# Taps of a depthwise convolution moved out of the B and C convolutions of an SSD, with four staging buffers for the memory products

## The chip, the cores and the metric

One core of one Trainium2 chip. The time is device microseconds (us) of one execution, as the median of several runs. A profile comes from one further, profiled execution. The engines are called PE (TensorE; PEld is its weight loading), DVE (VectorE), ACT (ScalarE), POOL (GpSimd) and SP (SyncE, which issues the transfers).

## What is computed

One decoder layer on 1024 tokens of width 1024, in float32 throughout. Cut to what matters here:

```
u = rms_norm(h); P = u @ W_in       # [conv GLU | z, x, B, C, dt | q, k, v | 3 gates]
y_A = conv_branch(...)              # a * sigmoid(gate), depthwise causal conv of 31 taps, LayerNorm, swish, W_A
y_B = ssd_branch(...)               # causal conv of 4 taps on x, B, C; chunked scan; silu(z); grouped norm; W_B
y_C = swa_branch(...)               # sliding-window attention
h += (sig(g_A)*y_A + sig(g_B)*y_B + sig(g_C)*y_C) @ W_mix
h += memory_cross_attention(rms_norm(h), rms_norm(mem))
h += relu(rms_norm(h) @ W_up)**2 @ W_down

# inside ssd_chunked, per group of 8 heads and chunk of 128 tokens
scores = (C @ B^T) * decay                      # decay = exp of differences of cumulated dt * a
y  = scores @ (x * dt)  +  (C @ state) * exp(cs)
state = state * exp(cs_end) + (B * decay_to_end)^T @ (x * dt)
```

## The kernel before

Every product of float32 operands is made of three matmuls on rounded halves: an operand is split into a high half (`wh`, `uh`) and a remainder (`wl`, `ul`), and hi*hi, hi*lo and lo*hi are added up in PSUM. A weight slot (`wslot`, L139 to L156) loads 128x1024 numbers into a staging tile `ws` (pool `wst`, 2 buffers), ACT rounds it into `wh` (L154) and POOL subtracts to get `wl` (L155); the halves come from the pool `wp`, of 3 buffers. `gemm_ch` (L191) makes 128 output channels of all 1024 tokens of it, in 8 steps of 6 matmuls with 512 columns.

The order on PE is the order of the program. Other engines get theirs from a scheduler, which may bring loads, casts and elementwise work forward; weight slots have high priority. Work that should lie between the matmuls is put in by hand: `step()` (L91) runs after a part of a product, and takes from a list of side jobs the first one that is due (`after(n, fn)` makes one due n steps from now). With each step it may also emit one tap of the depthwise convolution.

The taps: `convolve` (L316 to L335) is a generator. For each of 8 tiles of 128 channels it loads the GLU's result into `hin` (with POOL's memset of the left edge and ACT's first tap into `tapy`, L326), yields four times empty, and then emits 30 multiply-adds on DVE (L331, 128x1024 elements), one per yield. `pace[0]` says how often a step asks for one: with pace 2 every second step, with 3 every third, with 0 never. There is one `hin`, so a tile's load waits for the last tap of the tile before.

The stages:

- First (0 to about 125 us): x is loaded and split, three gate tiles are multiplied with the not yet normalised x as it comes (`ps_g`), the square sums give the norms of x and of the memory (`token_rstd`, L244; its steps are named `xn_...` and `mn_...`). Then the keys and values of the memory are made (`ps_kv`, L436 to L469): 16 weight slots of two loads of w_xkv of 256 KB each. Two of five of them take their halves from a pool `wkv` of WKV = 2 buffers, the others from `wp`, so there are five places for halves in all, and two staging tiles. Beside these products `normalise` (L410 to L421, due after 3 steps) multiplies x by its norm and splits it again: per tile DVE multiplies, ACT casts (`uh`) and DVE subtracts (`ul`).
- Second (about 125 to 640 us): the GLU tiles, k and v, q, z (L699 to L720). Taps run here with pace 2 (GLU, z) or 3 (k, v, q).
- SSD (about 640 to 1250 us): for each of four groups g there are four convolutions of 4 taps on x (`conv4`, L738: the product, an eviction by ACT into `c4v`, a first tap on ACT, three on DVE, L746, tanh on ACT, and DVE's L751), each turned to tokens by PE some 10 steps later (`to_tok`, L754, `ps_tok`). Then `b_and_c(g+1)` (L866) makes the next group's B and C in the same way, and `core(g)` (L774) does the chunks: PE multiplies C by the state (`ps_yo`), makes the state's increment (`ps_stt`) and the diagonal part (`ps_yd`); DVE copies or adds the state (L821, L819). `prepare(c)` loads the differences of the cumulated sums (`csb`), makes 8 relus and an exponential on ACT, masks them by `cbm` on DVE (L790), and makes `xd` (DVE, L792) and `xe` (POOL). Chunks 0 and 1 are prepared at the start of `core`, chunk c + 2 at the end of chunk c. Between the chunks `fill` makes parts of the gate tiles (`ps_g`). Taps run with pace 2 everywhere except in `core`, where the pace is 0.
- Then attention, the output products, the cross-attention and the MLP, which the change does not touch.

Of the kernel before, what the change touches and what calls it, by code (L numbers as in the profile page):

```python
# [17 lines left out]
P = 128  # L18
# [11 lines left out]

TURN, TURN_TOK, TURN_Y = 18, 10, 14
TURN_XQ = 8
WKV = 2
GCOL = 512


# [20 lines left out]
def trunk_kernel(tc, w_io):  # L57
# [3 lines left out]
    with ctx:  # L61
# [21 lines left out]
        side = []  # L83
        steps_done = [0]
        taps = [iter(())]
        pace = [0]

        def after(n, fn):
            side.append((steps_done[0] + n, fn))
# [1 line left out]
        def step():  # L91

            steps_done[0] += 1
            if pace[0] and steps_done[0] % pace[0] == 0:
                next(taps[0], 0)
            for i, (due, fn) in enumerate(side):
                if due <= steps_done[0]:
                    side.pop(i)
                    fn()
                    break  # L100
# [35 lines left out]
        d_bv = dram.tile([16, 384], F32, name="d_bv")  # L136
        d_skew = dram.tile([16, P * 385], F32, name="d_skew")

        def wslot(src, first=False, pool_=None):  # L139
            with ExitStack() as e:  # L140
                if not first:
                    e.enter_context(tc.high_priority())
                st = wst.tile([P, 1024], F32, tag="ws", name="ws")
                if isinstance(src, list):
                    for n, part in enumerate(src):
                        nc.sync.dma_start(
                            st.rearrange("p (k n c) -> p k n c", k=2, n=2)[:, :, n, :],
                            part.rearrange("p (k c) -> p k c", c=256),
                        )
                else:  # L150
                    nc.sync.dma_start(st, src)
                wh = (pool_ or wp).tile([P, 1024], F32R, tag="wh", name="wh")
                wl = (pool_ or wp).tile([P, 1024], F32R, tag="wl", name="wl")
                act.copy(wh, st)  # L154
                pool.tensor_sub(wl, st, wh.bitcast(F32))  # L155
            return wh, wl  # L156
# [117 lines left out]
        with ExitStack() as s1:  # L274
# [62 lines left out]
            with ExitStack() as sc:  # L337
# [58 lines left out]
                for i in range(NRAW):  # L396
# [7 lines left out]
                        else:  # L404
                            act.copy(th[:, h * 512:h * 512 + 512], fps[i][h])
                    raw.append(th)
                rm = token_rstd(xp, macc, M, 1.0 / D, EPS, "mn")
                pe.on = True

                def normalise():  # L410

# [18 lines left out]
                xv = xp.tile([P, 2, D], F32, name="xv")  # L430
                kt = memt.rearrange("p a b -> p (a b)").rearrange("p (a b) -> p a b", a=2)
                ss = xp.tile([P, 4, 2], F32, name="kss")
                wk = sc.enter_context(tc.tile_pool(name="wkv", bufs=WKV))
                after(3, normalise)
                after(26, raw_gates)
                for s in range(4):  # L436

                    ps = pg.tile([P, T], F32, tag="g", name="ps_kv").rearrange("p (a b) -> p a b", b=512)
                    for kp in range(4):
                        wh, wl = wslot(  # L440
                            [w_io["w_xkv"][s * 2 + n, kp // 2][:, kp % 2 * 512:kp % 2 * 512 + 512] for n in range(2)],
                            pool_=(wk, wk, None, None, None)[(s * 4 + kp) % 5],
                        )
                        for kk in range(2):
                            k = kp * 2 + kk
                            c = slice(kk * 512, kk * 512 + 512)
                            for tt in range(2):
                                a, b = mh[:, k, tt * P:(tt + 1) * P], ml[:, k, tt * P:(tt + 1) * P]
                                pe.matmul(ps[:, tt, :], a, wh[:, c], start=k == 0, stop=False)
                                pe.matmul(ps[:, tt, :], b, wh[:, c], start=False, stop=False)  # L450
                                pe.matmul(ps[:, tt, :], a, wl[:, c], start=False, stop=k == KT - 1)
                            step()
                    for tt in range(2):
                        to = kt if s < 2 else xv
                        v = to[:, tt, s % 2 * 512:s % 2 * 512 + 512]
                        act.activation(v, ps[:, tt, :], AF.Copy, scale=rm[:, tt:tt + 1])
                        if s < 2:
                            for h in range(2):
                                junk = x2.tile([P, 256], F32, tag="kjunk", name="kjunk", bufs=1)
                                act.activation(  # L460
                                    junk, v[:, h * 256:h * 256 + 256], AF.Square,
                                    accum_out=ss[:, s * 2 + h, tt:tt + 1],
                                )
                    if s == 1:
                        rk = rsqrt_small(xp, ss.rearrange("p a b -> p (a b)"), 8, 1.0 / 256, EPS, "rk")
                        for h in range(4):
                            for tt in range(2):
                                v = kt[:, tt, h * 256:(h + 1) * 256]
                                dve.tensor_scalar(v, v, rk[:, h * 2 + tt:h * 2 + tt + 1], None, ALU.mult)  # L469
# [26 lines left out]
            with ExitStack() as sc:  # L496
# [199 lines left out]
                            d_skew[h].rearrange("(q i) -> q i", i=385)[:, :384], d_bv[h].partition_broadcast(P)  # L696
                        )
                after(8, distances)
                pace[0] = 2  # L699
                glu(1)  # L700
                pace[0] = 3
                tm512(w_io["w_kv"], 0, keys_values)
                pace[0] = 2
                glu(2)
                pace[0] = 3
                tm512(w_io["w_q"], 0, queries_of(0))
                pace[0] = 2
                glu(3)
                pace[0] = 3
                tm512(w_io["w_q"], 1, queries_of(1))  # L710
                pace[0] = 2
                glu(4)
                tm512(w_io["w_z"], 0, z_of(0))
                steps()
# [9 lines left out]
            with ExitStack() as sc:  # L724
# [47 lines left out]
                    )  # L772

                def core(g, ctt):  # L774
                    state = None
                    ops = {}

                    def prepare(c):
                        col = c * 32 + g * HPG
                        hs = slice(col, col + HPG)  # L780
                        cb = fp.tile([P, HPG, P], F32, tag="csb", name="csb")
                        nc.sync.dma_start(
                            cb, d_cs[c, g * HPG:(g + 1) * HPG, :].rearrange("h q -> (h q)").partition_broadcast(P)
                        )
                        for r in range(HPG):
                            act.activation(
                                cb[:, r, :], cb[:, r, :], AF.Relu, bias=csc[:, col + r:col + r + 1], scale=-1.0
                            )
                        act.activation(cb, cb, AF.Exp, scale=-1.0)
                        dve.tensor_mul(cb, cb, cbm[:, c, :].unsqueeze(1).to_broadcast([P, HPG, P]))  # L790
                        xd = fp.tile([P, GCOL], F32, tag="xd", name="xd")
                        dve.tensor_mul(h3(xd), h3(xtok[:, c, :]), hb(dts[:, hs]))  # L792
                        xe = None
                        if c < NT - 1:
                            xe = fp.tile([P, GCOL], F32, tag="xe", name="xe")
                            pool.tensor_mul(h3(xe), h3(xtok[:, c, :]), hb(dtd[:, hs]))
                        pool.tensor_mul(h3(xtok[:, c, :]), h3(xtok[:, c, :]), hb(C("d_skip", g * HPG, HPG)))
                        ops[c] = cb, xd, xe

                    prepare(0)  # L800
                    prepare(1)
                    for c in range(NT):
# [28 lines left out]
                            dve.tensor_add(y, y, yo)  # L831
                        dve.tensor_add(y, y, pyd)
                        if c + 2 < NT:
                            prepare(c + 2)

                def finish(g):
# [33 lines left out]
                def turn_b(ctt):  # L870
                    to_tok(bt, btok)
                    for o in range(2):
                        after(TURN_TOK + o, lambda o=o: cb_of(ctt, o))

                ctt = b_and_c(0)
                turn_b(ctt)
                for g in range(4):
                    for j in range(4):
                        to_tok(
                            conv4(g * 4 + j), xtok[:, :, j * P:(j + 1) * P], (g - 1) * 4 + j if g else None  # L880
                        )
                    if g < 3:
                        following = b_and_c(g + 1)
                    else:
                        fill(TURN_TOK + 1)
                    pace[0] = 0
                    core(g, ctt)
                    pace[0] = 2
# [562 lines left out]
```

## Time and profile before

| | |
|---|---|
| median of 3 runs | 2826.53 us (2825.64 to 2829.45) |
| the profiled execution, its time / its span | 2829.2 us / 2827.4 us |
| mean granted clock of PE | 0.988 |
| idle time of PE in the span | 72.9 us |
| DVE, ACT, POOL busy | 50%, 36%, 30% |
| transfers | 267.22 MB, mean 95 GB/s |

The page gives busy times, a table of 40 slices and groups of instructions. A row of a timeline has the start in us, the duration, the engine, the line and operation, what is written and read, and in brackets the idle time of the engine before it with what ended it. "x4" is a run of four instructions, whose duration is that of the whole run. A row of the waits has who waited for whom, the total in us, how many times and the longest. A row of windows has the stretch and its length, the busy time (and instruction count) of PE, PEld, DVE, ACT and POOL, then the granted clock, the busy share of the DMA engines and GB/s.

### The profile page before, as it was taken

What the parts mean: (1) busy time and instruction counts of PE and PEld (TensorE: products, weight loads), DVE (VectorE), ACT (ScalarE), POOL (GpSimd) and SP (SyncE); (2) the same over time, 40 slices, a digit from 0 to 9 for tenths busy, and PEclk for the clock granted to TensorE, in tenths of its full rate; (3) what the DMA queues carried; (4) which work ended last, traced back from release to release, by engine and by line L of the source; (5) the groups of instructions that cost most, each with busy time, mean ns of one, the idle gap of its engine ahead of it and who ended that gap; (6) DMA issues with size and microseconds to landing.
All of it is one profiled execution on the core that took longest, in us unless ns stands there. A gap on an engine that the chain in (4) does not pass through costs nothing. (4 is left out here: it accounts for less than half of the span.)

```text
span 2827.4 us, 31802 instructions
## 1 busy us (share of the span) xinstructions
PE 2754.5 (97%) x12892; PEld 2221.7 (79%) x12892; DVE 1423.9 (50%) x1610; ACT 1004.3 (36%) x1662; POOL 843.2 (30%) x376
## 2 busy tenths in 40 slices
PE   8899999999899989999999999999999999999999
PEld 6688878888687868775578878899778888888887
DVE  6556667659788887755424674323342222222222
ACT  6523321124455546446612351336432211122111
POOL 4522221202526261524342332321142222222221
PEclk9999999999999999999999999999999999999999
DMA  6552232321333333352354332311111111111111
GB/s 215 183 143 90 88 119 94 103 89 60 103 114 107 102 104 120 114 188 83 101 201 163 113 105 89 105 53 39 45 45 45 45 52 46 45 53 45 53 45 75
DMA packets 94516, 267.22 MB, mean 95 GB/s; under 512 B 9105, under 2 KB 34081, under 8 KB 93985
## 3 DMA queue, kind: packets, MB, share of 16 engines
q1 hardware_dynamic: 94368, 265.19, 28.3%
q8 instruction: 101, 1.65, 0.2%
q14 instruction: 47, 0.38, 0.0%
HBM read 210.47 MB, written 57.83 MB: 95 GB/s over the span
## 5 line engine op out<-in xcount | busy, mean ns | idle before, releaser
L155 POOL TENSOR_TENSOR wl<-ws,wh 128x1024 fp32r<-128x1024 f32 x200 | 502.2, 2513 | 1387.1 <-ACT wh L154 1327.3
L74 PE MATMUL ps_g<-oh,wh 128*128 128x512 f32 x1792 | 563.1, 396 | 4.2 <-ACT oh L1037 4.2
L74 PE MATMUL ps_g<-ol,wh 128*128 128x512 f32 x1792 | 556.2, 392 | 3.7 <-DVE ol L1038 3.4
L74 PE MATMUL ps_g<-oh,wl 128*128 128x512 f32 x1792 | 553.8, 390 | 0.0
L154 ACT CAST wh<-ws 128x1024 fp32r<-128x1024 f32 x200 | 209.7, 1049 | 885.7 <-PE ps_g L74 777.3
L331 DVE SCALAR_TENSOR_TENSOR tapy<-hin,cst,tapy 128x1024 f32<-128x1024 f32 x240 | 396.2, 1651 | 30.7 <-ACT tapy L326 25.0
L74 PEld LDWEIGHTS ps_g<-oh,wh 128*128 128x128 f32 x1792 | 335.7, 188 | 80.8 <-issue 7.1
L74 PEld LDWEIGHTS ps_g<-ol,wh 128*128 128x128 f32 x1792 | 335.9, 188 | 80.3 <-DVE ol L1038 9.4
L74 PEld LDWEIGHTS ps_g<-oh,wl 128*128 128x128 f32 x1792 | 336.9, 188 | 72.0
L74 PE MATMUL ps_g<-uh,wh 128*128 128x512 f32 x1008 | 332.2, 408 | 9.3 <-ACT uh L350 8.2
L74 PE MATMUL ps_g<-ul,wh 128*128 128x512 f32 x1008 | 326.0, 398 | 0.1
L74 PE MATMUL ps_g<-uh,wl 128*128 128x512 f32 x1008 | 317.4, 394 | 1.7 <-POOL wl L155 1.7
L74 PEld LDWEIGHTS ps_g<-ul,wh 128*128 128x128 f32 x1008 | 191.1, 190 | 50.4 <-issue 9.3
L74 PEld LDWEIGHTS ps_g<-uh,wl 128*128 128x128 f32 x1008 | 191.0, 190 | 43.6 <-POOL wl L155 2.9
L74 PEld LDWEIGHTS ps_g<-uh,wh 128*128 128x128 f32 x1008 | 179.9, 191 | 38.3 <-ACT uh L350 8.2
L1341 DVE TENSOR_TENSOR ht<-ht,ps_g 128x1024 f32<-128x1024 f32 x64 | 78.2, 1222 | 250.2 <-PE ps_g L74 250.2
L74 PE MATMUL ps_tm<-wh,uh 128*128 128x512 f32 x448 | 175.7, 392 | 0.0
L74 PE MATMUL ps_tm<-wh,ul 128*128 128x512 f32 x448 | 174.6, 390 | 0.0
L74 PE MATMUL ps_tm<-wl,uh 128*128 128x512 f32 x448 | 174.4, 389 | 0.0
L1331 DVE SCALAR_TENSOR_TENSOR relu<-ps_g,rb 128x1024 f32<-128x1024 f32 x32 | 39.2, 1225 | 221.8 <-PE ps_g L74 221.8
L169 POOL TENSOR_TENSOR wl<-ws,wh 128x1024 fp32r<-128x1024 f32 x28 | 70.6, 2532 | 230.2 <-ACT wh L168 230.2
L746 DVE SCALAR_TENSOR_TENSOR c4a<-c4v,cst,c4a 128x1023 f32<-128x1023 f32 (+2 forms) x72 | 96.9, 1345 | 10.4 <-ACT c4a L744 9.0
(341 smaller groups left out, 3436.2 us busy)
## 6 DMA issues: line engine op xcount, KB each, us to landing
ws<-w_ch SPq DMA_DIRECT2D x64, 512.0 KB, 3.6
csb<-d_cs SPq DMA_DIRECT2D x32, 512.0 KB, 3.8
gth<-d_th SPq DMA_DIRECT2D x32, 512.0 KB, 4.4
ws<-w_up SPq DMA_DIRECT2D x32, 512.0 KB, 3.3
ws<-w_down SPq DMA_DIRECT2D x32, 512.0 KB, 3.3
d_th<-gate_th SPq DMA_DIRECT2D x21, 512.0 KB, 5.1
ws<-w_xkv SPq DMA_DIRECT2D x32, 256.0 KB, 3.1
ws<-w_z SPq DMA_DIRECT2D x16, 512.0 KB, 3.4
```

Of the source, the lines that this page charges most:

```text
L74: ins = nc.tensor.matmul(*a, **k)
L154: act.copy(wh, st)
L155: pool.tensor_sub(wl, st, wh.bitcast(F32))
L169: pool.tensor_sub(wl[:, :, c], s3, wh[:, :, c].bitcast(F32))
L331: dve.scalar_tensor_tensor(y, hin[:, j:j + T], w(j), y, ALU.mult, ALU.add)
L746: dve.scalar_tensor_tensor(a[:, s:], v[:, :T - s], C("c4_w", ct * 4 + 3 - s), a[:, s:], ALU.mult, ALU.add)
L1331: dve.scalar_tensor_tensor(r, ps, 0.0, rb, ALU.max, ALU.mult)
L1341: dve.tensor_add(hv, hv, ps)
```

## The change

- The memory products take one of four weight slots from the pool `wkv` (now of one buffer), the others from `wp`: four places for halves in place of five. Every second slot is staged in a tile of `wkv` instead of `wst`, with two buffers: four staging tiles in place of two.
- The norm of the memory (`mn`) becomes a side job that is due after one step, in place of standing ahead of the products.
- The pace becomes a fraction: each step adds it to `owed`, and a tap is emitted when that reaches 1. In the second stage it is 0.6 throughout (before 1/2 and 1/3), in the SSD 0.5 as before, and 0 from `b_and_c(g+1)` on (for the last group, from the `fill` in its place) to the end of `core`.
- `prepare` is cut in two: `exps(c)` loads `csb` and makes relus and exponential; for the first two chunks it is a side job, 2 and 6 steps into `b_and_c(g+1)`. For the others it stands at the old place, ahead of `prepare(c + 2)`.

```diff
             steps_done[0] += 1
-            if pace[0] and steps_done[0] % pace[0] == 0:
+            owed[0] += pace[0]
+            if owed[0] >= 1:
+                owed[0] -= 1
                 next(taps[0], 0)
...
-        def wslot(src, first=False, pool_=None):
+        def wslot(src, first=False, pool_=None, stage=None):
...
-                st = wst.tile([P, 1024], F32, tag="ws", name="ws")
+                st = (stage or wst).tile([P, 1024], F32, tag="ws", name="ws", bufs=2 if stage else None)
...
-                rm = token_rstd(xp, macc, M, 1.0 / D, EPS, "mn")
                 pe.on = True
+                rms = []
+                after(1, lambda: rms.append(token_rstd(xp, macc, M, 1.0 / D, EPS, "mn")))
...
-                wk = sc.enter_context(tc.tile_pool(name="wkv", bufs=WKV))
+                wk = sc.enter_context(tc.tile_pool(name="wkv", bufs=1))
...
-                            pool_=(wk, wk, None, None, None)[(s * 4 + kp) % 5],
+                            pool_=wk if (s * 4 + kp) % 4 == 0 else None, stage=wk if kp % 2 else None,
...
-                pace[0] = 2
+                pace[0] = 0.6
                 glu(1)
-                pace[0] = 3
                 tm512(w_io["w_kv"], 0, keys_values)
...
+                    pace[0] = 0
+                    do = core(g, ctt)
+                    for c in range(2):
+                        after(2 + 4 * c, lambda c=c: do.exps(c))
                     if g < 3:
                         following = b_and_c(g + 1)
                     else:
                         fill(TURN_TOK + 1)
-                    pace[0] = 0
-                    core(g, ctt)
-                    pace[0] = 2
+                    do.run()
+                    pace[0] = 0.5
                     finish(g)
```

How the instructions move is shown at three places. The first is DVE in group 0 of the SSD, from the last steps of the first x convolution (`c4a`, of four steps each) to the third; `tapy` rows are taps, `cbm` and `csb` the mask and the masked decays. Before:

```order
L751 SCALAR_TENSOR_TENSOR c4a<-c4v,c4a 128x1024
L331 SCALAR_TENSOR_TENSOR tapy<-hin,cst,tapy 128x1024
L769 TENSOR_TENSOR cbm<-ps_cb,mat 128x512
L790 TENSOR_TENSOR csb<-csb,cbm 128x1024
L746 SCALAR_TENSOR_TENSOR c4a<-c4v,cst,c4a 128x1023
L746 SCALAR_TENSOR_TENSOR c4a<-c4v,cst,c4a 128x1022
L746 SCALAR_TENSOR_TENSOR c4a<-c4v,cst,c4a 128x1021
L751 SCALAR_TENSOR_TENSOR c4a<-c4v,c4a 128x1024
L331 SCALAR_TENSOR_TENSOR tapy<-hin,cst,tapy 128x1024 x3
```

The same place of DVE now:

```order
L747 SCALAR_TENSOR_TENSOR c4a<-c4v,c4a 128x1024
L332 SCALAR_TENSOR_TENSOR tapy<-hin,cst,tapy 128x1024
L765 TENSOR_TENSOR cbm<-ps_cb,mat 128x512
L332 SCALAR_TENSOR_TENSOR tapy<-hin,cst,tapy 128x1024
L790 TENSOR_TENSOR csb<-csb,cbm 128x1024
L332 SCALAR_TENSOR_TENSOR tapy<-hin,cst,tapy 128x1024 x2
L742 SCALAR_TENSOR_TENSOR c4a<-c4v,cst,c4a 128x1023
L742 SCALAR_TENSOR_TENSOR c4a<-c4v,cst,c4a 128x1022
L742 SCALAR_TENSOR_TENSOR c4a<-c4v,cst,c4a 128x1021
L747 SCALAR_TENSOR_TENSOR c4a<-c4v,c4a 128x1024
L332 SCALAR_TENSOR_TENSOR tapy<-hin,cst,tapy 128x1024 x4
```

Between the first and second convolution stand four taps where one stood, since the four empty yields between two channel tiles of the taps have moved; behind the second, four where three stood.

The second place is DVE in the same group, from the end of the last x convolution to the state of the first chunk; `bt` is B's last step, and the `c4a` rows behind it are C's. Before:

```order
L331 SCALAR_TENSOR_TENSOR tapy<-hin,cst,tapy 128x1024 x4
L746 SCALAR_TENSOR_TENSOR c4a<-c4v,cst,c4a 128x1023
L792 TENSOR_TENSOR xd<-xtok,dtmp_dt 128x512
L746 SCALAR_TENSOR_TENSOR c4a<-c4v,cst,c4a 128x1022
L792 TENSOR_TENSOR xd<-xtok,dtmp_dt 128x512
L746 SCALAR_TENSOR_TENSOR c4a<-c4v,cst,c4a 128x1021
L751 SCALAR_TENSOR_TENSOR bt<-c4v,c4a 128x1024
L331 SCALAR_TENSOR_TENSOR tapy<-hin,cst,tapy 128x1024 x4
L746 SCALAR_TENSOR_TENSOR c4a<-c4v,cst,c4a 128x1023
L746 SCALAR_TENSOR_TENSOR c4a<-c4v,cst,c4a 128x1022
L821 COPY state<-ps_stt 128x512
```

The same place of DVE now:

```order
L742 SCALAR_TENSOR_TENSOR c4a<-c4v,cst,c4a 128x1023
L792 TENSOR_TENSOR xd<-xtok,dtmp_dt 128x512
L742 SCALAR_TENSOR_TENSOR c4a<-c4v,cst,c4a 128x1022
L792 TENSOR_TENSOR xd<-xtok,dtmp_dt 128x512
L742 SCALAR_TENSOR_TENSOR c4a<-c4v,cst,c4a 128x1021
L747 SCALAR_TENSOR_TENSOR bt<-c4v,c4a 128x1024
L742 SCALAR_TENSOR_TENSOR c4a<-c4v,cst,c4a 128x1023
L742 SCALAR_TENSOR_TENSOR c4a<-c4v,cst,c4a 128x1022
L830 COPY state<-ps_stt 128x512
```

The eight taps are gone from this stretch; all else is in its old order.

The third place is the start of the program on SP, where `ws` rows are loads of weights and `xt` rows loads of x. Before:

```order
L108 DMA cst<-consts 128x582
L151 DMA ws<-w_ch 128x1024
L349 DMA xt<-xT 128x1024
L151 DMA ws<-w_ch 128x1024
L349 DMA xt<-xT 128x1024 x2
L151 DMA ws<-w_ch 128x1024
L146 DMA ws<-w_xkv 128x2x256 x2
```

The same place of SP now:

```order
L147 DMA ws<-w_xkv 128x2x256 x4
L109 DMA cst<-consts 128x582
L152 DMA ws<-w_ch 128x1024
L350 DMA xt<-xT 128x1024
L152 DMA ws<-w_ch 128x1024
L350 DMA xt<-xT 128x1024
L152 DMA ws<-w_ch 128x1024
```

The four loads for the new staging tiles, which wait for nothing, have moved to the head of the queue. The loads of `csb` and the relus and exponentials of the first two chunks stand at nearly the same places on SP and ACT as before, where the scheduler had already put them ahead.

More of the change, by code (lines that the diff above doesn't have):

```diff
@@ L32 @@
 TURN_XQ = 8
-WKV = 2
 GCOL = 512
@@ L85, in trunk_kernel @@
         taps = [iter(())]
-        pace = [0]
+        pace, owed = [0], [0]
         def after(n, fn):
@@ L455, in trunk_kernel @@
                         v = to[:, tt, s % 2 * 512:s % 2 * 512 + 512]
-                        act.activation(v, ps[:, tt, :], AF.Copy, scale=rm[:, tt:tt + 1])
+                        act.activation(v, ps[:, tt, :], AF.Copy, scale=rms[0][:, tt:tt + 1])
                         if s < 2:
@@ L698, in trunk_kernel @@
                 after(8, distances)
-                pace[0] = 2
+                pace[0] = 0.6
                 glu(1)
-                pace[0] = 3
                 tm512(w_io["w_kv"], 0, keys_values)
-                pace[0] = 2
                 glu(2)
-                pace[0] = 3
                 tm512(w_io["w_q"], 0, queries_of(0))
-                pace[0] = 2
                 glu(3)
-                pace[0] = 3
                 tm512(w_io["w_q"], 1, queries_of(1))
-                pace[0] = 2
                 glu(4)
@@ L774, in core, with exps @@
                 def core(g, ctt):
-                    state = None
-                    ops = {}
-                    def prepare(c):
+                    cbs, ops = {}, {}
+                    def exps(c):
                         col = c * 32 + g * HPG
-                        hs = slice(col, col + HPG)
                         cb = fp.tile([P, HPG, P], F32, tag="csb", name="csb")
@@ L789, in prepare @@
                         act.activation(cb, cb, AF.Exp, scale=-1.0)
+                        cbs[c] = cb
+                    def prepare(c):
+                        hs = slice(c * 32 + g * HPG, c * 32 + (g + 1) * HPG)
+                        cb = cbs.pop(c)
                         dve.tensor_mul(cb, cb, cbm[:, c, :].unsqueeze(1).to_broadcast([P, HPG, P]))
@@ L798, in prepare, with run @@
                         ops[c] = cb, xd, xe
+                    class do:
+                        pass
+                    do.exps = exps
+                    do.run = lambda: run(g, ctt, ops, exps, prepare)
+                    return do
+                def run(g, ctt, ops, exps, prepare):
+                    state = None
                     prepare(0)
@@ L833, in core @@
                         if c + 2 < NT:
+                            exps(c + 2)
                             prepare(c + 2)
@@ L885, in trunk_kernel @@
                         fill(TURN_TOK + 1)
-                    pace[0] = 0
-                    core(g, ctt)
-                    pace[0] = 2
+                    do.run()
+                    pace[0] = 0.5
                     finish(g)
```

## Prediction

> **What bounds the kernel now.** I read the page first (busy times, the 40 slices), then the list of waits of TensorE, then the timelines around the longest of them.
>
> ```profile
> span 2827.4 us, 31802 instructions
> PE 2754.5 (97%) x12892; PEld 2221.7 (79%) x12892; DVE 1423.9 (50%) x1610; ACT 1004.3 (36%) x1662; POOL 843.2 (30%) x376
> L331 DVE SCALAR_TENSOR_TENSOR tapy<-hin,cst,tapy 128x1024 f32<-128x1024 f32 x240 | 396.2, 1651 | 30.7 <-ACT tapy L326 25.0
> ```
>
> TensorE (PE) is busy 2754.5 of 2827.4 us, and the change takes no matmul away. All that can be had is idle time of PE (2827.4 - 2754.5 = 72.9 us) and matmuls that run slower than they need to behind it. The 240 taps of the depthwise convolution on VectorE (DVE) cost 1651 ns each on the mean, and by the tap's own line (least, median, most) 1271 to 3487:
>
> ```profile
> L331 DVE SCALAR_TENSOR_TENSOR tapy<-hin,cst,tapy x240: 1271/1285/3487, 156.6 to 1230.5; 128x1024 f32<-128x1024 f32 x120
> ```
>
> The waits of PE (total, times, longest) name who ends its idle time:
>
> ```profile
> PE ps_yo L74 <- DVE state L821: 19.3, 3, 7.7
> PE ps_kv L74 <- POOL wl L155: 4.8, 3, 2.8
> PE ps_kv L74 <- DVE mn_a L235: 4.2, 1, 4.2
> PE ps_tok L78 <- DVE c4a L751: 2.4, 2, 1.4
> PE ps_yd L74 <- DVE xd L792: 2.1, 1, 2.1
> ```
>
> The largest stands in the SSD core, at the second chunk of a group: PE waits for the state that DVE copies out of PSUM. PE's timeline in group 0 (start, duration, instruction; in brackets the idle time before it):
>
> ```profile
> 714.34 1.02 PE L74 MATMUL ps_stt<-xe,btok 128*128 128x512 f32 x2
> 715.19 1.89 PE L74 MATMUL ps_yd<-xd,csb 128*128 128x64 f32 x16
> ...
> 728.89 2.05 PE L74 MATMUL ps_yo<-state,ctt 128*128 128x512 f32 x2 [7.64 <-DVE state L821]
> 741.01 1.02 PE L74 MATMUL ps_yo<-state,ctt 128*128 128x512 f32 x2
> 748.65 1.02 PE L74 MATMUL ps_yo<-state,ctt 128*128 128x512 f32 x2
> 749.50 1.02 PE L74 MATMUL ps_stt<-xe,btok 128*128 128x512 f32 x2
> 756.28 1.02 PE L74 MATMUL ps_yo<-state,ctt 128*128 128x512 f32 x2
> ```
>
> and DVE's at the same place:
>
> ```profile
> 717.58 8.05 DVE L331 SCALAR_TENSOR_TENSOR tapy<-hin,cst,tapy 128x1024 f32<-128x1024 f32 x4
> 725.55 2.60 DVE L746 SCALAR_TENSOR_TENSOR c4a<-c4v,cst,c4a 128x1023 f32<-128x1023 f32 x2
> 728.06 0.69 DVE L821 COPY state<-ps_stt 128x512 f32<-128x512 f32 x1
> ```
>
> The product that the copy reads (ps_stt) was there at 714.34 + 1.02 = 715.4. The copy ran at 728.06, behind four taps of 8.05 us and two steps of the C convolution.
>
> **The core without that wait.** Undisturbed chunks follow each other every 756.28 - 748.65 = 7.63 us, and from a chunk's ps_stt to the next chunk's ps_yo are 756.28 - 749.50 = 6.78 us. So from the first chunk's ps_stt to the third chunk's ps_yo it should be 6.78 + 7.63 = 14.41. Group 0 took 741.01 - 714.34 = 26.67: 12.3 too much, of which 7.64 is idle time and the rest a PE that starts again slowly (its ps_yo takes 2.05 in place of 1.02). The other groups:
>
> ```profile
> 861.74 1.02 PE L74 MATMUL ps_stt<-xe,btok 128*128 128x512 f32 x2
> 882.99 1.02 PE L74 MATMUL ps_yo<-state,ctt 128*128 128x512 f32 x2
> 1005.08 1.02 PE L74 MATMUL ps_stt<-xe,btok 128*128 128x512 f32 x2
> 1029.89 1.02 PE L74 MATMUL ps_yo<-state,ctt 128*128 128x512 f32 x2
> 1143.54 1.02 PE L74 MATMUL ps_stt<-xe,btok 128*128 128x512 f32 x2
> 1146.68 2.78 PE L74 MATMUL ps_yd<-xd,csb 128*128 128x64 f32 x16 [2.13 <-DVE xd L792]
> 1155.91 1.02 PE L74 MATMUL ps_yo<-state,ctt 128*128 128x512 f32 x2
> ```
>
> Group 1: 21.25 - 14.41 = 6.8. Group 2: 24.81 - 14.41 = 10.4. In group 3 the wait comes earlier, before ps_yd, and is over by the second chunk: 12.37 - 6.78 = 5.6. Together 35.1 us. The change emits no tap while the next group's B and C convolutions are multiplied, and DVE's order of the changed kernel has none from the last x convolution to the state copy, in all four groups. The copy then stands behind the B convolution and two steps of the C convolution only; two such steps took 2.60, so without the 8.05 of taps it would have been done by 728.06 - 8.05 + 0.69 = 720.7, and PE wants it at 714.34 + 6.78 = 721.1. That looks close, but all of DVE's work ahead of it was late as well: four more taps went between the last x convolution and B. I take the whole 35.1, and as the lower bound 35.1 less one wait of 4 us in each of three groups, 23.
>
> **What the taps cost in their new place.** A first part goes into the projections before the SSD (one tap in 0.6 of the steps, before 1/2 and 1/3).
>
> ```profile
> 125.00:640.00 515.00, 515.00 (x2315) 423.90 (x2315) 317.90 (x307) 140.13 (x176) 119.25 (x51) 1.00 0.32 106
> ```
>
> PE has no gap there, DVE is free for 515 - 317.9 = 197 us. Some 30 taps more at 1.65 are 50 us, so DVE goes from 62 to about 71% on the mean; the steps that PE needs from it are due many steps later. I put this at 0, with 3 us of waits as the bad end. [...]
>
> The second part is new: in group 0 three more taps stand between the first two x convolutions and one more between the second and third. DVE and PE there:
>
> ```profile
> 668.95 3.91 DVE L746 SCALAR_TENSOR_TENSOR c4a<-c4v,cst,c4a 128x1023 f32<-128x1023 f32 x3
> 675.19 6.07 DVE L331 SCALAR_TENSOR_TENSOR tapy<-hin,cst,tapy 128x1024 f32<-128x1024 f32 x3
> 687.42 7.38 DVE L331 SCALAR_TENSOR_TENSOR tapy<-hin,cst,tapy 128x1024 f32<-128x1024 f32 x4
> 676.28 0.60 PE L78 MATMUL ps_tok<-mat,c4a 128*128 128x128 f32 x4
> 688.10 0.60 PE L78 MATMUL ps_tok<-mat,c4a 128*128 128x128 f32 x4
> 701.11 0.66 PE L78 MATMUL ps_tok<-mat,c4a 128*128 128x128 f32 x4 [1.03 <-DVE c4a L751]
> ```
>
> The convolution that starts at 668.95 was done at about 675.2, where the taps behind it start, one us ahead of the ps_tok that turns it (676.28). Three taps more are 3 x 1.28 to 3 x 1.65 = 3.8 to 5.0 us, so PE waits about 2.8 to 4. From there DVE needs four taps and a convolution per conv, 687.42 to 701.1 = 13.6 us, where PE needs 688.10 - 676.28 = 11.8: another 1.7 at each of the next two. That is 6.6 us of waits, less the 1.03 that was there already: 5.6. I take 5, and 2.5 to 9 as bounds, the upper with a slow start of 3.4 behind the longest wait. The row for that is 1146.68: after 2.13 us of idle time its ps_yd took 2.78 (the one at 715.19 took 1.89), where the row with 1.03 us of idle time shows next to nothing of it (0.66 for 0.60). [...]
>
> **The start.** The memory products wait for a normaliser chain and a raw copy on DVE; then they run slowly for 13 matmuls:
>
> ```profile
> 52.77 0.77 PE L74 MATMUL ps_kv<-wh,mh 128*128 128x512 f32 x1 [4.19 <-DVE mn_a L235]
> 53.34 0.63 PE L74 MATMUL ps_kv<-wh,ml 128*128 128x512 f32 x1
> 58.87 0.39 PE L74 MATMUL ps_kv<-wl,mh 128*128 128x512 f32 x1
> 59.10 0.39 PE L74 MATMUL ps_kv<-wh,mh 128*128 128x512 f32 x1
> 65.88 3.43 DVE L419 SCALAR_TENSOR_TENSOR xt<-xt,cst,rb 128x1024 f32<-128x1024 f32 x1
> ```
>
> From 53.34 to 58.87 are 13 matmuls at 0.425 us, then 0.23 apart: 13 x 0.2 = 2.6 lost, with the gap 6.8. The norm of the memory moves on by a step, and the memory's own load is issued earlier, as SP no longer stands at a weight's buffer ahead of it; I count the 6.8 as won, with 0 as the other end (DVE's order keeps the raw copies, which really end this wait, ahead of the norm). Against it, SP now issues four loads of w_xkv, 1 MB, before the first weight and the first x.
>
> ```profile
> 0.00:50.00 50.00, 39.77 (x164) 31.88 (x164) 32.05 (x30) 33.72 (x46) 21.36 (x17) 1.00 0.69 244
> 1.18 0.42 SPq L151 DMA_DIRECT2D ws<-w_ch  x1
> ```
>
> The transfers move 244 GB/s at a busy share of 0.69, 354 GB/s when busy: 1.05 MB are 3.0 us, and nothing hides them, since PE waits for x at the start. Bounds: 4 issues of 0.42 = 1.7, and 1.05 MB at 244 = 4.3. After that the weights have one place less and DVE takes three multiplications, then three subtractions, where it alternated before, so the casts behind them on ACT are later by one DVE instruction, 1.2 to 3.4 us each (3.43 is one that met a subtraction of GpSimd; the taps, of the same shape and kind, take 1.27 to 1.28 alone). The waits for wl grow by that: I take 3.4, bounds 0 and twice 3.4. In sum 6.8 - 3.0 - 3.4 = +0.4; bounds +10 (the 4.8 for wl also gone) and -11.
>
> **The sum.** 35.1 - 5 + 0.4 = 30.5 us. The profiled execution took 2829.2 us (span 2827.4), 2.7 above the median of 2826.53; I take the gain off the median: **2796 us**. The exponentials themselves I cost at nothing: their loads and casts stand at the same places on SP and ACT as before, since the scheduler had already brought them forward.
>
> **The rivals.**
> 1. The start goes wrong. The 1 MB costs 4.3, the first wait stays, and the waits for wl double: -8 to -11 in place of +0.4. The time is 2805. For it: the load order puts the weights ahead of x, and x is what PE waits for. Against it: the 4.19 gap is the largest of that stage.
> 2. All goes well. The new waits in group 0 are 2.5 and the start gains 9: 35.1 - 2.5 + 9 = 41.6, 2785. For it: four staging buffers let SP run ahead.
> 3. It doesn't do what it says. If the state is late for another reason (the loads and exponentials of csb, or GpSimd's xe and dec), the taps' leaving only shows the next wait, and the core gains 10 to 15 of 35: about 2816 to 2821 with the 5 of group 0. Against it: the 8.05 us of taps ahead of the copy are larger than the 7.64 of idle time.
> 4. Slower. VectorE becomes the bound of the projections: the taps put there meet GpSimd's subtractions at 3.4 us and push the evictions of the q and z products late, so that PE waits in its stage without gaps. That decides from the point at which DVE needs over 197 us more there; 30 taps at 3.4 are 102. To be slower than now PE would have to wait over 36 us: e.g. the 8 q turns and 4 kv turns each by 3.4 = 41, so 2826 - 30.5 + 41 = 2837. Against it: no gap at all now, at 62% DVE.
>
> **How the numbers follow.** A measurement of this kernel tells about 0.2% (5.7 us) from no change. The forecast has 0.62 (2788 to 2802), rival 1 0.15, rival 2 0.12, rival 3 0.07 (of which 0.04 within 0.2%), rival 4 0.04. Faster: 0.62 + 0.15 + 0.12 + 0.03 = 0.92, same 0.04, slower 0.04. The range takes in rivals 1 and 2 with their bounds, 2784 to 2811; 3 and 4 and some tail are left out.
>
> **What would show it.** Right: in the waits of PE the line ps_yo <- state is gone or below 2 us, ps_yd <- xd too, and yo follows stt by 6.8 in all groups; ps_tok <- c4a rises from 2.4 to about 8; the first matmul starts at 11 rather than 8.2 us; no gap from 125 to 640 us. Wrong: state still named for several us (rival 3), any gap of PE between 125 and 640 (rival 4), the memory products ending later than before by over 5 us (rival 1). Time after 1270 us should be the same to within 1 us, shifted.

## The result, and the profile after

| | before | after |
|---|---|---|
| median | 2826.09 us (4 runs, 2819.73 to 2829.45) | 2793.49 us (4 runs, 2792.15 to 2796.37) |
| span of the profiled execution | 2827.4 us | 2793.0 us |
| ratio of the runs | | 0.9889, 95% interval 0.9869 to 0.9908 |

The change takes 32.6 us off the median (30.5 forecast) and 34.4 off the profiled span. The page of the changed kernel, its first lines:

```profile
span 2793.0 us, 31816 instructions
PE 2737.7 (98%) x12892; PEld 2211.6 (79%) x12892; DVE 1430.1 (51%) x1610; ACT 1005.0 (36%) x1662; POOL 839.4 (30%) x376
```

PE's idle time fell from 72.9 to 2793.0 - 2737.7 = 55.3 us, by 17.6; its busy time fell by 16.8, with the same 12892 matmuls, and its mean granted clock rose from 0.988 to 0.994 (a loss of 0.012 x 2827 = 33.9 us before and of 0.006 x 2793 = 16.8 now). Half of the gain is thus not idle time but matmuls that no longer start slowly behind it. Of the waits of PE in the changed kernel (total, times, longest), those ahead of attention:

```profile
PE ps_g L73 <- ACT uh L351: 11.5, 1, 11.5
PE ps_kv L73 <- POOL wl L156: 7.0, 2, 5.1
PE ps_tok L77 <- DVE c4a L747: 5.7, 3, 3.0
PE ps_kv L73 <- ACT wh L155: 3.1, 2, 2.6
PE ps_g L73 <- POOL wl L156: 0.3, 1, 0.3
```

The lines of ps_yo and ps_yd are gone, and so is that of ps_kv for the norm. The first wait, for x, went from 8.2 to 11.5, those for the memory weights and for the turned convolutions rose. PE and then DVE in group 0's core:

```profile
715.73 1.02 PE L73 MATMUL ps_stt<-xe,btok 128*128 128x512 f32 x2
722.48 1.02 PE L73 MATMUL ps_yo<-state,ctt 128*128 128x512 f32 x2
730.12 1.02 PE L73 MATMUL ps_yo<-state,ctt 128*128 128x512 f32 x2
```

```profile
713.05 1.23 DVE L747 SCALAR_TENSOR_TENSOR bt<-c4v,c4a 128x1024 f32<-128x1024 f32 x1 [1.19 <-ACT c4v L745]
716.17 3.40 DVE L742 SCALAR_TENSOR_TENSOR c4a<-c4v,cst,c4a 128x1023 f32<-128x1023 f32 x2 [1.90 <-ACT c4a L740]
719.50 0.68 DVE L830 COPY state<-ps_stt 128x512 f32<-128x512 f32 x1
```

From ps_stt to the third chunk's ps_yo are 730.12 - 715.73 = 14.39 us, the undisturbed 14.41. The copy is done at 720.2, and PE takes it at 722.5: 2.3 us of slack. The other groups, first ps_stt and third chunk's (in the last group second chunk's) ps_yo:

```profile
850.56 1.02 PE L73 MATMUL ps_stt<-xe,btok 128*128 128x512 f32 x2
864.95 1.02 PE L73 MATMUL ps_yo<-state,ctt 128*128 128x512 f32 x2
986.80 1.02 PE L73 MATMUL ps_stt<-xe,btok 128*128 128x512 f32 x2
1001.18 1.02 PE L73 MATMUL ps_yo<-state,ctt 128*128 128x512 f32 x2
1114.83 1.02 PE L73 MATMUL ps_stt<-xe,btok 128*128 128x512 f32 x2
1121.58 1.02 PE L73 MATMUL ps_yo<-state,ctt 128*128 128x512 f32 x2
```

14.39, 14.38 and 6.75 (undisturbed 14.41 and 6.78): no group loses anything here any more. Where the time went shows best from places that both programs pass, each the first PE instruction of its kind:

| place | before | after | difference |
|---|---|---|---|
| first matmul | 8.20 | 11.46 | +3.3 |
| first memory product (ps_kv) | 52.77 | 50.70 | -2.1 |
| first turned convolution (ps_tok) | 650.79 | 646.53 | -4.3 |
| first chunk of group 0 (ps_stt) | 714.34 | 715.73 | +1.4 |
| attention (ps_lg) | 1243.46 | 1207.92 | -35.5 |
| end of the span | 2827.4 | 2793.0 | -34.4 |

The start won 4.3 us, the convolutions of group 0 gave back 5.7, the SSD from there to attention won 36.9.

### The profile page after: what moved, and what is told of

Its sections match the earlier page's. It is cut to its first block, busy times and chain, and to the rows that moved or that the text cites. A ratio compares the mean times of both kernels' runs of the same rounds, so it can differ in the third digit from the quotient of the medians.

```text
span 2793.0 us, 31816 instructions
## 1 busy us (share of the span) xinstructions
PE 2737.7 (98%) x12892; PEld 2211.6 (79%) x12892; DVE 1430.1 (51%) x1610; ACT 1005.0 (36%) x1662; POOL 839.4 (30%) x376
## 5 line engine op out<-in xcount | busy, mean ns | idle before, releaser
L332 DVE SCALAR_TENSOR_TENSOR tapy<-hin,cst,tapy 128x1024 f32<-128x1024 f32 x240 | 389.9, 1625 | 31.0 <-ACT tapy L327 24.7
L73 PE MATMUL ps_g<-uh,wh 128*128 128x512 f32 x1008 | 330.6, 407 | 11.5 <-ACT uh L351 11.5
L73 PEld LDWEIGHTS ps_g<-uh,wh 128*128 128x128 f32 x1008 | 178.9, 190 | 39.7 <-ACT uh L351 11.5
```

The source lines that it names most:

```text
L73: ins = nc.tensor.matmul(*a, **k)
L332: dve.scalar_tensor_tensor(y, hin[:, j:j + T], w(j), y, ALU.mult, ALU.add)
```

## The experiments

The kernel before and the changed kernel are taken apart first, then the changed kernel is bent in single places. Each ratio is taken against runs of the kernel before that were made beside it. Their median was 2826.05 us for the first four experiments, 2824.16 for the two taps in the B and C convolutions and the last three, and 2825.71 for the others.

### The taps out of the B and C convolutions, alone

```diff
+                    pace[0] = 0
                     if g < 3:
                         following = b_and_c(g + 1)
                     else:
                         fill(TURN_TOK + 1)
-                    pace[0] = 0
                     core(g, ctt)
```

> The kernel before, with one line moved: no taps during the next group's B and C convolutions (integer paces, start and exponentials as before). Theory (taps ahead of the state copy are the whole stall): the gap before ps_yo is gone in all groups, the core gains 35 us, nothing new in group 0 (one tap, not four, between its first two x convolutions). The some 35 taps left over run behind group 3, beside attention's start, and give back 0 to 10 there: 2791 to 2802. Rival (exponentials or GpSimd are late as well): the gap stays in part, and the gain is below 15 us, 2811 or more.

Measured 2819.06 us, ratio 0.9978 (0.9966 to 0.999): 7 us. The part of the theory on the core held. No wait of ps_yo or ps_yd is left, and attention begins at 1209.63, 33.8 us earlier than before. The part on the left-over taps failed, by far: 0 to 10 us were expected for them. The longest waits of PE are now in attention:

```profile
PE ps_pt L78 <- POOL lg L968: 12.9, 5, 6.8
PE ps_lg L74 <- DVE mx L949: 9.3, 3, 7.8
```

and DVE at the start of attention:

```profile
1206.60 11.22 DVE L331 SCALAR_TENSOR_TENSOR tapy<-hin,cst,tapy 128x1024 f32<-128x1024 f32 x7 [15.78 <-ACT tapy L326]
1218.83 0.29 DVE L949 CUSTOM_DVE_ANT_0 lg<-ps_lg,bias 128x128 f32<-128x128 f32 x1 [1.01 <-DMA d_yb<-yt]
1219.05 1.28 DVE L331 SCALAR_TENSOR_TENSOR tapy<-hin,cst,tapy 128x1024 f32<-128x1024 f32 x1
1220.24 0.28 DVE L949 CUSTOM_DVE_ANT_0 lg<-ps_lg,bias 128x128 f32<-128x128 f32 x1
```

A whole channel tile of 30 taps runs here. A step of attention that adds the bias takes 0.28 us, and behind each stands a tap of 1.28. From ps_lg to attention's output product (the first `ps_g<-oh`) the kernel before takes 1243.46 to 1409.4 = 165.9 us, this one 1209.63 to 1401.9 = 192.3: 26.4 us given back. So the removal of the taps wins 34 and their arrival in attention costs 26. What makes the change pay is the 0.6 of the second stage, which the prediction put at a cost of 0 and never at a worth.

### The exponentials, alone

The kernel before with `exps(0)` and `exps(1)` split off from `prepare` and emitted as side jobs of `b_and_c`, paces as before.

```diff
+                    do = core(g, ctt)
+                    for c in range(2):
+                        after(2 + 4 * c, lambda c=c: do.exps(c))
                     if g < 3:
                         following = b_and_c(g + 1)
```

> The kernel before, with the exponentials of the first two chunks split off and emitted in the B and C convolutions, taps there as before. Theory: the scheduler had them there already, so nothing changes: 2826, within 3, and ps_yo still waits for the state, 19 us in all. Rival (the exponentials' place is part of the gain): 7 to 20 us faster, and the waits of ps_yo below 15.

Measured 2824.66 us, ratio 0.9999 (0.9988 to 1.001). PE's waits are still led by the state:

```profile
PE ps_yo L74 <- DVE state L834: 19.3, 3, 7.6
```

That is 19.3 us in three waits, as before. This part of the change does nothing.

### The start, alone

The kernel before with four staging tiles, the new places for halves and the later norm.

```diff
-                            pool_=(wk, wk, None, None, None)[(s * 4 + kp) % 5],
+                            pool_=wk if (s * 4 + kp) % 4 == 0 else None, stage=wk if kp % 2 else None,
```

> The kernel before, with the new staging tiles, weight places and norm alone. Theory: the first matmul is 3.3 us later, the wait at the first memory product is gone, and the first stage ends some 4 us earlier, as in the whole change: 2822. Rival (the start's gain in the whole change comes from elsewhere, the taps' new pace): 2826 or more.

Measured 2820.55 us, ratio 0.9984 (0.9974 to 0.9993): 5.5 us. Its first ps_tok stands at 646.62, that of the whole change at 646.53: the start's gain is the same with either set of taps.

### The changed kernel with the norm back ahead

```diff
-                after(1, lambda: rms.append(token_rstd(xp, macc, M, 1.0 / D, EPS, "mn")))
+                rms = [token_rstd(xp, macc, M, 1.0 / D, EPS, "mn")]
```

> The changed kernel, with the memory's norm ahead of the memory products again. Theory: the wait ended with the raw copy, and that is early now because the memory is loaded earlier, so the norm's place does nothing: within 1.5 us of the changed kernel (2792 to 2795). Rival (the norm's move removed the wait of 4.2 us and the slow start behind it): 4 to 7 us slower than the changed kernel, with a gap at the first memory product.

Measured 2793.40 us, ratio 0.9887 (0.9868 to 0.9907), against 2793.49 of the changed kernel. The first memory product has no gap (51.53 us), so the norm's new place does nothing. The rows also tell what PE waited for in the kernel before:

```profile
48.62 1.23 DVE L258 TENSOR_TENSOR xacc<-mat,xn_r 128x1024 f32<-128x1024 f32 x1
50.01 1.29 DVE L404 COPY raw<-ps_g 128x512 f32<-128x512 f32 x2 [0.17 <-PE ps_g L73]
51.53 0.48 PE L73 MATMUL ps_kv<-wh,mh 128*128 128x512 f32 x1
51.71 0.16 DVE L236 TENSOR_SCALAR mn_a<-ps_st 128x2 f32<-128x2 f32 x1 [0.41 <-PE ps_st L73]
```

PE begins the memory products before the norm's first step, `mn_a`, although the norm stands ahead of them in the program, as it did in the kernel before. So it does not need the norm. What it needs from DVE are the raw copies, as the prediction said, and in the kernel before these ended late, at 52.62, with PE's first memory product at 52.77 (50.56 and 50.70 in the changed kernel):

```profile
48.06 3.37 DVE L257 TENSOR_TENSOR xacc<-mat,xn_r 128x1024 f32<-128x1024 f32 x1
51.35 1.27 DVE L403 COPY raw<-ps_g 128x512 f32<-128x512 f32 x2
```

The instruction ahead of them (`xacc`, which spreads x's norm) took 3.37 us, beside a subtraction of POOL that began at 48.00. It takes 1.23 here, as POOL's subtraction begins only at its end, at 49.76: the cast that this one needs waited on ACT for PE to free a place of the halves (48.63, 1.10 us of idle time). All four traces with the old start show 3.36 to 3.37 us, all six with the new one 1.23. The changed kernel's first memory product is 2.1 us earlier, as much as that instruction is shorter; the rest of the 4.19 us went since PE comes to this place 2 us later. The load of the memory is issued earlier too (32.57 us before, 29.36 in the changed kernel), but DVE's chain for x's norm (`xn_a`) did not begin earlier by it, at 46.10 and 46.38.

### Both parts of the taps' move, without the start

The changed kernel with WKV, the two staging tiles and the norm as before.

> The changed kernel with its start undone (staging, places for halves and norm as before): the taps' move with both its halves, more of them in the second stage and none in the B and C convolutions. Theory (the two parts add up, and the 0.6 pace is what keeps the left-over taps out of attention): 2793.5 + 4 to 5.5 = 2797.5 to 2799, with no wait of ps_yo for the state and none of attention for taps. Rival (the start and the taps hang together, as the start alone measured 5.5): below 2795 or above 2802.

Measured 2798.14 us, ratio 0.9898 (0.9881 to 0.9915). The parts add up: 27.6 us by the taps and 5.5 by the start make 33.1, and the change measured 32.6. Against the first experiment, which differs from this one in the second stage's pace (and the exponentials, which did nothing alone), the pace is worth 2819.06 - 2798.14 = 20.9 us: attention takes 165.0 us again (1212.94 to 1377.97).

### Two taps in the B and C convolutions

```diff
-                    pace[0] = 0
+                    pace[0] = 0.25
                     do = core(g, ctt)
...
+                    pace[0] = 0
                     do.run()
```

> The changed kernel, with a pace of 0.25 in the B and C convolutions in place of 0 (two taps ahead of B's last steps and two ahead of the state copy in groups 0 and 1, two in group 2, none in group 3, where the taps are done). Theory (the state copy comes 2.3 us after it could and 2.3 us before PE wants it, 720.2 against 722.5; a tap takes 1.3 to 2): two taps ahead of it use up the slack and 0.3 to 2 us more, in two groups, with a slow start at most: 2794 to 2800, and a short wait of ps_yo on the state. Rival (the stall goes with the number of taps from the first one on, half of 35 us): 2807 to 2812.

Measured 2800.59 us, ratio 0.9918 (0.9903 to 0.9933): 7.1 slower than the changed kernel by the medians (8.2 by the ratios), 0.6 above the range of the theory and 6 below that of the rival. DVE and PE in group 0:

```profile
716.09 5.38 DVE L332 SCALAR_TENSOR_TENSOR tapy<-hin,cst,tapy 128x1024 f32<-128x1024 f32 x2
721.38 2.59 DVE L742 SCALAR_TENSOR_TENSOR c4a<-c4v,cst,c4a 128x1023 f32<-128x1023 f32 x2
723.89 0.68 DVE L830 COPY state<-ps_stt 128x512 f32<-128x512 f32 x1
```

```profile
715.29 1.02 PE L73 MATMUL ps_stt<-xe,btok 128*128 128x512 f32 x2
724.72 1.12 PE L73 MATMUL ps_yo<-state,ctt 128*128 128x512 f32 x2 [2.52 <-DVE state L830]
734.09 1.02 PE L73 MATMUL ps_yo<-state,ctt 128*128 128x512 f32 x2
```

The two taps took 5.38 us, with POOL at work beside both (one took 3.39, the other 1.95; the median tap of the changed kernel takes 1.285). With the two taps ahead of B's last steps they pushed the copy from 719.50 to 723.89. The slack was used up and PE idled 2.52; with the slow start from ps_stt to the third chunk are 18.80 us, 4.4 too many. In group 1 two taps of 5.40 us stand at the same place, but DVE had B's last step 2.4 us ahead of ps_stt (852.15, 854.54) and not 0.4 (714.94, 715.29): the wait is 0.50 us and the loss 0.7. In group 2 the taps are done before B's last steps, and no wait is left. The stall does not go with the number of taps: it begins where the slack ends.

### All taps in the second stage

```diff
-                pace[0] = 0.6
+                pace[0] = 1
```

> The changed kernel with a pace of 1 in place of 0.6 in the second stage: all 240 taps are then in that stage, none in the SSD. Theory (rival 4 of the prediction has its point somewhere above 0.6): a q turn takes eight taps of 1.28 us and some 8 us of other work of DVE in 11 us of PE, so over the eight q turns DVE falls behind by some 50 us, of which the slack of the evictions takes 24: PE waits 10 to 40 us in the second stage, and 6 us of waits in the SSD go: 2797 to 2828. Rival (DVE's mean load decides, 390 + 60 x 1.6 = 486 of 515 us, and the slack takes the rest): no gap in the second stage and 2787 to 2789.

Measured 2842.47 us, ratio 1.0054 (1.0038 to 1.0071): slower than the kernel before. PE's new waits:

```profile
PE ps_g L73 <- DVE zth L588: 13.9, 3, 9.2
PE ps_qt L77 <- DVE qtok L526: 12.3, 4, 7.0
PE ps_tm L73 <- DVE glu_th L311: 5.8, 2, 5.2
```

and its second stage, by engine (PE, PEld, DVE, ACT, POOL):

```profile
125.00:640.00 515.00, 476.21 (x2073) 386.36 (x2072) 406.72 (x370) 123.54 (x150) 119.45 (x52) 0.96 0.31 100
```

PE idles 38.8 us in that window, and its clock is 0.96 on the mean, by which (1 - 0.96) x 515 = 20.6 us more are lost. The first ps_tok comes at 703.01, 56.5 us later than at 0.6. This is the prediction's rival 4, at a pace of 1 instead of 0.6, and its place (q and z) was right, with the GLU's eviction as a third. The expectation's 10 to 40 us took in the idle time, but not the slow starts behind it. DVE's mean load (79%) says nothing of it: the eviction of z (`zth`) at 458.75 stood behind eight taps in a row, of 16.51 us. From the first ps_tok to the first chunk of group 0 are 62.3 us here, in place of 69.2, as no tap is left there.

### Fewer taps in group 0

```diff
                 for g in range(4):
+                    pace[0] = 0.3 if g == 0 else 0.5
                     for j in range(4):
```

> The changed kernel, with a pace of 0.3 in place of 0.5 in the x convolutions of group 0 alone. Theory (four taps and a convolution are 13.6 us on DVE where PE needs 11.8): the waits of 2.99 and 1.51 us before ps_tok go, and with them 4 to 6 us: 2788 to 2790. Rival (the taps only move on and cost the same in group 2 or in attention): 2793, with new waits there.

Measured 2787.34 us, ratio 0.9859 (0.9843 to 0.9874), just below the theory's 2788 to 2790. No wait of ps_tok is left that is over a microsecond, the convolutions follow each other by 11.8 us, and from the first ps_tok (646.55) to the first chunk (708.85) are 62.3 us in place of 69.2. The last tap runs at 1163.0, still ahead of attention. This beats both kernels: 6.2 us below the changed one.

### No w_xkv ahead of x

The changed kernel, with the first two staged weights issued without priority.

```diff
+                            first=s == 0 and kp % 2 == 1,
                             pool_=wk if (s * 4 + kp) % 4 == 0 else None, stage=wk if kp % 2 else None,
```

> The changed kernel, with the first two staged weights of the memory products issued without priority, so that no load of w_xkv stands ahead of the first x. Theory (the 1 MB costs the 3.3 us by which the first matmul came later): the first matmul is back at 8.2 us and 2 to 3.3 us of it reach the end: 2790 to 2791.5. Rival (the later start is made up before the memory products, which wait for their own chain anyway): within 1 us of the changed kernel, 2793, with a new gap at the first memory product.

Measured 2793.37 us, as the changed kernel: neither the theory nor the rival fits it whole. The first matmul is earlier as the theory had it (8.72 us), and so is the first memory product (48.32, from 50.70), but at the first ps_tok 0.8 us of that are left and at attention 1.7. The medians don't show them.

With the fewer taps of group 0 as well:

> The changed kernel with both edits tried so far, fewer taps in group 0 and no w_xkv ahead of x. Theory (the memory products are bound by DVE, GpSimd and ACT, so an earlier start is lost there): as with the fewer taps alone, 2786 to 2789. Rival (the two add up): 2784 to 2785.5.

Measured 2788.93 us, ratio 0.9879 (0.9864 to 0.9893), beside 2787.34 without the later loads. In the trace the first ps_tok comes 3.8 us earlier (642.76 against 646.55) and attention 2.4 (1197.67 against 1200.10), and the span is still 3.7 longer, 2785.6 against 2781.9. Where those 6.1 us went is in the last section. Whether the earlier start pays at the end stays open.

### Normalisation in turn

The kernel with fewer taps in group 0, with DVE's multiplication and subtraction of each tile of x kept in program order.

```diff
-                        dve.scalar_tensor_tensor(xt, xt, C("g_mix", k), rb, ALU.mult, ALU.mult)
+                        tc.keep_in_program_order(
+                            dve.scalar_tensor_tensor(xt, xt, C("g_mix", k), rb, ALU.mult, ALU.mult)
+                        )
```

> The kernel with fewer taps in group 0, and in the normalisation of x DVE's multiplications and subtractions kept in turn, tile by tile. Theory (the casts of the weights stand on ACT behind casts of x that wait for the next multiplication, and that stands behind three subtractions of 3.4 us): the waits of the memory products for wh and wl (8 us) fall below 3, and 4 to 6 us of it reach the end: 2781 to 2784. Rival (DVE and GpSimd are in each other's way in any order): 2786 to 2788.

Measured 2790.34 us, ratio 0.9882 (0.9867 to 0.9896): not faster than without it (2787.34), above the rival's 2786 to 2788 too, and the first ps_tok is 3.2 us later. The theory falls. Its DVE and POOL:

```profile
72.12 3.44 DVE L422 SCALAR_TENSOR_TENSOR xt<-xt,cst,rb 128x1024 f32<-128x1024 f32 x1
76.68 2.23 DVE L426 TENSOR_TENSOR ul<-xt,uh 128x1024 fp32r<-128x1024 f32 x1 [1.12 <-ACT uh L424]
```

```profile
67.76 23.50 POOL L156 TENSOR_TENSOR wl<-ws,wh 128x1024 fp32r<-128x1024 f32 x7 [4.62 <-ACT wh L155]
```

Seven subtractions of POOL in a row took 23.50 us, 3.36 each, while DVE's instructions beside them took 3.44 and 2.23 and waited for a cast in between. In turn, nearly every instruction of DVE in this stretch meets one of POOL: ahead of those seven, at 66.42 and 65.28, a multiplication took 1.27 and a subtraction 1.21. The casts are earlier, and one long wait for a weight (5.2 us of 7.3 in three) became a short one at nearly every weight (4.1 us in eight, the longest 1.8).

All three edits together:

> All three edits: fewer taps in group 0, normalisation in turn, no w_xkv ahead of x. Theory (with the memory products no longer bound by casts the earlier start comes through): 2 to 3 us below the normalisation in turn without it, 2779 to 2782, the first matmul at 8.2 to 8.8 us. Rival (the start is lost again before or in the memory products): the same as without it, within 1 us.

Measured 2786.96 us, ratio 0.9867 (0.985 to 0.9883). That is 3.4 below the same without the earlier loads of x, where 2 to 3 were expected, but the single runs of the two overlap (2784.53 to 2788.72 and 2787.74 to 2792.97). It is not at 2779 to 2782: the step that the normalisation was to win is missing, and the first matmul stands at 9.32, not at 8.2 to 8.8. It is level with the fewer taps alone.

## Why the prediction was right, point by point

- **The sum: 30.5 forecast, 32.6 measured by the medians.** By the trace its three terms make 36.9 - 5.7 + 4.3 = 35.5, 5 more than forecast. The medians show less, since 1.1 us are lost again from attention on and the profiled execution of the kernel before was 3.1 us above its median, that of the changed kernel 1.3. So the sum came nearer than its terms, and the start is the term that was mis-sized most.
- **The core: 35.1 forecast, 35.1 + 1.8 measured.** All four groups now run at their undisturbed distance, and the way of working it out (an undisturbed distance of the same program, taken off the disturbed one) carried the slow starts along without a term of their own. The remaining 1.8 are of later steps of the SSD. Alone, and with the taps sent to attention, the same removal was worth 7.
- **The new waits in group 0: 5 forecast, 5.7 measured, in part by luck.** The wait at the second convolution was 2.99 (2.8 to 4 forecast) and one of 1.51 stood where two of 1.7 were forecast. With the 1.03 of before taken off, the waits grew by 3.5 only, and over the whole kernel from 2.4 to 5.7 and not to 8. What brought the loss to 5.7 is mostly a slow start, which the forecast had in its upper bound alone. Behind the longest wait PE started like this:

```profile
675.42 0.66 PE L77 MATMUL ps_tok<-mat,c4a 128*128 128x128 f32 x4 [2.99 <-DVE c4a L747]
675.83 1.03 PE L73 MATMUL ps_g<-uh,wh 128*128 128x512 f32 x2
679.79 0.63 PE L73 MATMUL ps_g<-ul,wh 128*128 128x512 f32 x2
```

  A pair that takes 0.63 took 1.03, for some 3.5 us, in which pairs start 0.85 apart in place of 0.46: some 1.6 us are lost behind this wait of 2.99 us. The upper bound had 3.4 us for a slow start; group 3 of the kernel before had lost 5.6 - 2.13 = 3.5 beside its wait of 2.13 us.
- **The start: +0.4 forecast, +4.3 measured in the trace and 5.5 by the median of the start alone.** Right were 3.3 us for the four loads ahead of x (3.0 forecast) and the first wait and its slow start gone. The waits for memory weights grew from 4.8 + 1.7 to 7.0 + 3.1, by 3.6 (3.4 forecast), which agrees less well than it looks: in the six traces with this start they are 7.9 to 10.3 us, in the four with the old one 6.5 to 7.1. That the first wait would go was right for another reason than the two given, the norm's new place and the memory's earlier load: an instruction of DVE no longer meets one of POOL (1.23 us in place of 3.37, see the experiment with the norm back ahead), which is luck. Left out was the end of the stage, where the kernel before waited for the weights of the first GLU tile:

```profile
113.58 0.73 PE L74 MATMUL ps_g<-uh,wh 128*128 128x512 f32 x2 [1.07 <-ACT wh L154]
116.02 0.73 PE L74 MATMUL ps_g<-uh,wl 128*128 128x512 f32 x2 [1.24 <-POOL wl L155]
```

  Of these 0.3 us is left, and from the first memory product to the first ps_tok are 595.8 us in place of 598.0. The cause given for the longer waits, casts that stand behind the normalisation's, is in the trace, DVE's three subtractions of 3.4 us (the first and the last are shown) and the cast of x behind them:

```profile
75.87 3.39 DVE L423 TENSOR_TENSOR ul<-xt__472,uh 128x1024 fp32r<-128x1024 f32 x1
82.54 3.41 DVE L423 TENSOR_TENSOR ul<-xt,uh 128x1024 fp32r<-128x1024 f32 x1
85.88 2.47 DVE L421 SCALAR_TENSOR_TENSOR xt<-xt,cst,rb 128x1024 f32<-128x1024 f32 x2
```

```profile
87.18 1.05 ACT L422 CAST uh<-xt 128x1024 fp32r<-128x1024 f32 x1 [6.46 <-DVE xt L421]
89.33 1.04 ACT L155 CAST wh<-ws 128x1024 fp32r<-128x1024 f32 x1
```

  The experiment shows that another order of them wins nothing; by its rows what binds there is DVE and POOL together.
- **The second stage: 0 forecast, 0 measured.** DVE's busy time went up from 317.9 to 389.2 us, by 71 (50 forecast), since 42 taps more run there and not 30, and PE still has no gap:

```profile
125.00:640.00 515.00, 515.00 (x2316) 423.79 (x2315) 389.18 (x349) 139.99 (x176) 123.54 (x53) 1.00 0.33 108
```

  The experiment with a pace of 1 (406.72 us) shows how near the edge lies.
- **The exponentials: nothing forecast, nothing measured.** Nor does the norm's place do anything.
- **Not seen:** that the left-over taps would have cost 26 us in attention without the new pace. The sum came out since the change moves both together; a forecast of the first half alone would have been wrong by 20 us, and the expectation for it was.

## What to carry to other kernels

Work that fills an engine's idle time must be priced at three places: where it leaves, where it goes now, and where the remainder ends when there is no room left; here 34 us won at the first could have been 7 in all. What decides is the slack of the next thing in that engine's queue (2.3 us here), not its mean load: two taps were too many at 51% of DVE over the whole span, and pace 1 too fast at 79% in its stage. And the releaser that a wait names need not be what has to move: the profile named the norm, but PE waited for the copies ahead of it, and these stood behind an instruction that had met POOL (3.37 us in place of 1.23).

## What the runs showed of the hardware

PE starts slowly behind waits, but not by the same amount each time. Attention ends with waits of 3.44 and of 3.8 to 4.3 us in every kernel here, by the same instructions. From the first ps_lg to the first output product the kernel with fewer taps took 1200.10 to 1364.6 = 164.5 us, the one with x first as well 1197.67 to 1365.5 = 167.8, where the two programs do the same. The windows around it, first of the one and then of the other (behind the busy times stands the clock):

```profile
1350.00:1375.00 25.00, 16.78 (x78) 9.32 (x76) 8.07 (x12) 12.91 (x30) 4.18 (x2) 0.93 0.66 206
1375.00:1400.00 25.00, 24.51 (x101) 19.88 (x102) 7.60 (x7) 5.28 (x6) 14.91 (x7) 0.93 0.68 257
```

```profile
1350.00:1375.00 25.00, 16.75 (x69) 9.77 (x68) 6.48 (x10) 12.28 (x30) 3.60 (x1) 0.86 0.64 195
1375.00:1400.00 25.00, 24.44 (x93) 19.31 (x94) 8.39 (x7) 6.08 (x6) 14.42 (x7) 0.86 0.70 268
```

Busy times are alike, the clock is 0.93 in the one and 0.86 in the other. From 1300 to 1325 it is 1.00 and 0.93. A difference of 0.07 over 25 us is 1.75 us; the two windows up to the output product make 3.5, where 3.3 more were measured, and the one behind it makes 1.75 more. From 2050 to 2150, where both have a wait of 1.05 us, the clock is 1.00 and 0.98: another 2. Together that is about 7 us, beside the 6.1 that went: the same waits cost more in the one execution than in the other. The spread between single executions of one kernel (2783.72 to 2788.37 us for the one with fewer taps) is of this size, so a gain of 2 us at the start can be read at a place in the trace, but not in a median of four runs.
